# State-space phase powers for eight groups at once, one tap operand for real and imaginary part, the relu's square on ScalarE

## The chip, the core and the metric

The kernel runs on one core of a Trainium2 chip. Its time is the device time of one execution in microseconds (us). Engines are named as the profile names them: PE is TensorE's matmuls and PEld its weight loads, DVE is VectorE, ACT is ScalarE, POOL is GpSimd, SP is SyncE, which issues most of this kernel's transfers (DMA).

## The reference, cut to what matters

Two blocks of a network run one after the other on 512 tokens of width 1024, beside 256 context tokens. The change lies in the first block: in its squared-relu MLPs, and in what is prepared for the second layer's state-space (S5) mixer.

```python
def squared_relu_mlp(h, w1, w2):
    return jnp.square(jax.nn.relu(h @ w1)) @ w2

def s5_discretize(a_re, a_im, b_re, b_im, c_re, c_im, log_dt):
    ...
    a_bar = jnp.exp(dt * a)
    b_bar = ((a_bar - 1) / a)[..., None] * lax.complex(f(b_re), f(b_im))
    c_mat = lax.complex(f(c_re), f(c_im))
    return a_bar, b_bar, c_mat

def s5_scan(u, a_bar, b_bar, c_mat, x0):
    ...   # x[t] = a_bar * x[t-1] + b_bar u[t];  y[t] = Re(c_mat x[t]), 64 groups of 16 channels, 64 states
```

## The kernel before

**Stages.** In layer 0 a projection (w_out, `out_proj`, 8 column blocks) ends the first mixer; then comes the MLP of layer 0 (`mlp(0, ...)`) on all 768 tokens, the S5 mixer of layer 1, the MLP of layer 1 on 512 tokens, and the second network block. Each column block of a projection is one call of `lin`: a weight tile is loaded (SP), split into a high part `wh` (ACT, L250) and a low part `wl` (POOL, L258), and multiplied in three matmuls for each of 8 row blocks (L287, L288, L289), once for tokens 0 to 511 and once for 512 to 767. The results lie in PSUM tiles `mm`, four of them: two column blocks of 768 tokens.

**The MLP.** It goes in four quarters. A quarter makes 8 hidden tiles from w1 and then 8 column blocks of w2, whose results are added onto the stream by DVE (L507). A hidden tile is made for each token range from its `mm` tile: relu into `x` (ACT, L539), its square rounded into `fh` (ACT, L540), the full-precision square `max(mm, 0) * x` into `x` (DVE, L541, which reads `mm` again and so is the last to free it), and then, over both ranges, `fl = x - fh` (DVE, L258).

**S5 preparation.** While w_out and the MLP of layer 0 run, a generator does other work in small steps: `tick` is called after each `lin` and advances `background` by 91/66 of a step. Steps alternate between a column of layer 1's modulation (`ada`, DVE L377) and a step of `s5_prep`; after 32 columns all steps are `s5_prep`'s. It goes over 64 groups in fours (GB = 4), 16 passes, and for each pass:

- `ca`: powers times C, two complex products of 320 columns (24 DVE instructions with `pp` below); their imaginary part is negated (ACT, L695), both parts go to DRAM (`dQ`). Parts of both are copied into the zero-padded `z` (`s_cz`, ACT, L698 and L699), which has room for the real and the imaginary part. Eight matmuls `sw` (L704) multiply `z` by B: four with the real, four with the imaginary part, added in one PSUM tile.
- `W` (`s_w`): the tile evicted (ACT, L706), a diagonal added (DVE, L707), and sent to DRAM (`dT`) in 32 small transfers (SP, L710).
- `pp`: powers times B (DVE), transposed on PE into `st` (L721, real and imaginary part after each other), evicted into the one buffer `s_pt` (ACT, L722) and sent to DRAM (`dP`).
- `E` (`s_e`): the powers 0 to 96 of the unit phase, by doubling: seven complex products, each of six DVE instructions in `cmul` (L575 to L582), 4 groups by 1, 2, 4, 8, 16, 32 and 32 powers; then one transfer (`dE`).

The generator is empty after 66 of the 72 calls of `lin`. The S5 mixer begins with matmuls into `y` (L754), whose PSUM space is that of the preparation's tiles.

**Order.** The instructions' order on each engine is set when the program is built, by a scheduler that simulates times of its own; it runs over the whole program. On the chip each engine then goes in that order and waits where it has to.

Of the kernel before, what the change touches and what calls it, by code (L numbers as in the profile page):

```python
# [14 lines left out]
AF = mybir.ActivationFunctionType  # L15
OP = mybir.AluOpType
# [194 lines left out]
class Prog:  # L211
# [309 lines left out]
    def mlp(self, l, xs, nt, r, raw=None):  # L521
        nc = self.nc
        with ExitStack() as es:
            self.pp = es.enter_context(self.pool(f'psF{l}', space=PSUM, bufs=1))
            hp = es.enter_context(self.pool(f'hF{l}', side='right'))
            fp = es.enter_context(self.pool(f'hid{l}', side='right'))
            with ExitStack() as e2:
                self.slabs = 2
                hs = self.norm_mod(fp, hp, xs, nt, l, 1, r)
            for q in range(4):  # L530
                hid = []
                for u in range(8):
                    ps = self.lin(self.I['mlp_w1'][l, q * 8 + u], hs, nt)
                    r = self.slab(fp)
                    h = self.t(fp, [128, NT], 'fh', F32R, self.hid_bufs)
                    lo = self.t(fp, [128, NT], 'fl', F32R, self.hid_bufs)
                    for p, (g, o, n) in zip(ps, self.groups(nt)):
                        s = slice(o, o + n)
                        nc.scalar.activation(r[:, s], p[:, :n], AF.Relu)  # L539
                        nc.scalar.activation(h[:, s], r[:, s], AF.Square)  # L540
                        nc.vector.scalar_tensor_tensor(r[:, s], p[:, :n], 0.0, r[:, s], op0=OP.max, op1=OP.mult)  # L541
                    self.lo(lo[:, :nt], r[:, :nt], h[:, :nt])
                    hid.append((h, lo))
                st = Stat(self, [self.slab(fp) for _ in range(2)], nt) if q == 3 else None
                self.out_proj(self.I['mlp_w2'][l, q], hid, xs, nt, lambda c, g: self.mod[l][:, 40 + c, g:g + 1], st, raw if st else None)
            return st.end(fp)
# [37 lines left out]
    def s5_prep(self):  # L584

        nc, I, tc = self.nc, self.I, self.tc
        G = 64
        v = nc.vector
        sp = self.sp
# [11 lines left out]
        k = small('k')  # L601
# [60 lines left out]
        B = self.GB  # L662
# [4 lines left out]
        self.dR = dd('dR', [128, G])  # L667
        nc.sync.dma_start(self.dR, rho)
        self.dE = [dd(f'dE{i}', [128, 2, 8, 97]) for i in range(nb)]
        z = self.t(sp, [128, 2, B, 15, 16], 's_cz')  # L670
        nc.gpsimd.memset(z, 0.0)
        id16 = self.const('id16', pool=sp)
        N = 8
        bb = self.t(sp, [128, 2, N + 1, 16], 's_bb')
        nc.gpsimd.memset(bb[:, :, N], 0.0)
        yield
        for g0 in range(0, G, B):
            i, g8 = g0 // 8, slice(g0 % 8, g0 % 8 + B)
            g = slice(g0, g0 + B)
            if g0 % N == 0:  # L680
                b = self.t(sp, [128, 2, N, 16], 's_b')
                gn = slice(g0, g0 + N)
                nc.sync.dma_start(b, I['s5_b'][:, :, gn])
                bc = lambda x: x[:, gn, None].to_broadcast([128, N, 16])
                self.cmul(sp, (bb[:, 0, :N], bb[:, 1, :N]), (b[:, 0], b[:, 1]), (bc(cf[0]), bc(cf[1])), [128, N, 16], conj_tag='s_t')
                yield
            n0 = g0 % N
            c = self.t(sp, [128, 2, B, 16], 's_cc')
            nc.sync.dma_start(c, I['s5_c'][:, :, g])
            ca = self.t(sp, [128, 2, B, 10, 16], 's_ca')  # L690
            tk = lambda x: x[:, :, g].rearrange('p k g -> p g k')[:, :, :, None].to_broadcast([128, B, 10, 16])
            ck = lambda j: c[:, j, :, None, :].to_broadcast([128, B, 10, 16])
            for h in (slice(0, 5), slice(5, 10)):
                self.cmul(sp, (ca[:, 0, :, h], ca[:, 1, :, h]), (ck(0)[:, :, h], ck(1)[:, :, h]), (tk(PW[0])[:, :, h], tk(PW[1])[:, :, h]), [128, B, 5, 16], conj_tag='s_t')
            nc.scalar.activation(ca[:, 1], ca[:, 1], AF.Copy, scale=-1.0)  # L695
            for r in range(2):
                nc.sync.dma_start(self.dQ[i][:, r, g8], ca[:, r, :, 1:9].rearrange('p g t h -> p g (t h)'))
            nc.scalar.activation(z[:64, :, :, 7:], ca[:64, :, :, 0:8], AF.Copy)  # L698
            nc.scalar.activation(z[64:, :, :, :8], ca[64:, :, :, 2:10], AF.Copy)  # L699

            ps = ps_('sw')
            for r in range(2):
                for u in range(B):
                    nc.tensor.matmul(ps[32 * u:32 * u + 32, :240], bb[:, r, n0 + u:n0 + u + 2].rearrange('p g h -> p (g h)'), z[:, r, u].rearrange('p k h -> p (k h)'), start=r == 0, stop=r == 1)  # L704
            W = self.t(sp, [128, 15, 16], 's_w')
            nc.scalar.activation(W.rearrange('p t h -> p (t h)'), ps[:, :240], AF.Copy)  # L706
            v.scalar_tensor_tensor(W[:, 7], id16, self.pk('s5_d')[:, g0 // B:g0 // B + 1], W[:, 7], op0=OP.mult, op1=OP.add)  # L707
            for u in range(B):
                for s_ in range(8):
                    nc.sync.dma_start(self.dT[i][s_ * 16:s_ * 16 + 16, g0 % 8 + u], W[32 * u:32 * u + 16, 7 - s_:15 - s_].rearrange('p t h -> p (t h)'))  # L710
            yield
            pp = self.t(sp, [128, 2, B, 8, 16], 's_ca')
            tk = lambda x: x[:, :, g].rearrange('p k g -> p g k')[:, :, :, None].to_broadcast([128, B, 8, 16])
            ck = lambda j: bb[:, j, n0:n0 + B, None, :].to_broadcast([128, B, 8, 16])
            for h in (slice(0, 4), slice(4, 8)):
                self.cmul(sp, (pp[:, 0, :, h], pp[:, 1, :, h]), (ck(0)[:, :, h], ck(1)[:, :, h]), (tk(PP[0])[:, :, h], tk(PP[1])[:, :, h]), [128, B, 4, 16], conj_tag='s_t')
            for r in range(2):
                pt = self.t(sp, [128, B, 128], 's_pt')
                ps = ps_('st')
                for n in range(B):  # L720
                    nc.tensor.transpose(ps[:, n * 128:n * 128 + 128], pp[:, r, n].rearrange('p s h -> p (s h)'), self.ident)  # L721
                nc.scalar.activation(pt.rearrange('p g q -> p (g q)'), ps, AF.Copy)  # L722
                nc.sync.dma_start(self.dP[i][:, r, g8], pt)
            yield
            E = self.t(sp, [128, 2, B, 97], 's_e')
            nc.gpsimd.memset(E[:, 0, :, 0:1], 1.0)
            nc.gpsimd.memset(E[:, 1, :, 0:1], 0.0)
            for r in range(2):
                nc.gpsimd.tensor_copy(E[:, r, :, 1:2], ph[r][:, g, None])
            n = 1  # L730
            while n < 96:
                m = min(n, 96 - n)
                self.cmul(sp, [E[:, r, :, n + 1:n + 1 + m] for r in range(2)], [E[:, r, :, 1:1 + m] for r in range(2)],
                          [E[:, r, :, n:n + 1].to_broadcast([128, B, m]) for r in range(2)], [128, B, m], conj_tag='s_t')
                n += m
            nc.sync.dma_start(self.dE[i][:, :, g8], E)
            yield

    def s5_mixer(self, xs, xpx, x2x, r):
# [1388 lines left out]
```

## Time and profile before

| what | us |
|---|---|
| median of 3 timed runs (3776.2 to 3780.95) | 3779.33 |
| the profiled execution, its own time | 3774.4 |
| its span, first to last instruction | 3772.6 |
| PE busy (18415 matmuls) | 3457.0 (92%) |
| DVE busy (5101 instructions) | 2665.1 (71%) |
| ACT busy (2484) | 1531.7 (41%) |
| POOL busy (810) | 1263.9 (34%) |

The busy shares are means over stages that are limited by different things. So the profile is read by stage: for a stretch of time, how long each engine was busy, what PE waited for in it, and what clock PE was granted (1.00 is 2.4 GHz, 0.5 is 1.2 GHz).

### The profile page before, as it was taken

What the parts mean: (1) busy time and instruction counts of PE and PEld (TensorE: products, weight loads), DVE (VectorE), ACT (ScalarE), POOL (GpSimd) and SP (SyncE); (2) the same over time, 40 slices, a digit from 0 to 9 for tenths busy, and PEclk for the clock granted to TensorE, in tenths of its full rate; (3) what the DMA queues carried; (4) which work ended last, traced back from release to release, by engine and by line L of the source; (5) the groups of instructions that cost most, each with busy time, mean ns of one, the idle gap of its engine ahead of it and who ended that gap; (6) DMA issues with size and microseconds to landing.
All of it is one profiled execution on the core that took longest, in us unless ns stands there. A gap on an engine that the chain in (4) does not pass through costs nothing. (4 is left out here: it accounts for less than half of the span.)

```text
span 3772.6 us, 50694 instructions
## 1 busy us (share of the span) xinstructions
PE 3457.0 (92%) x18415; PEld 2923.8 (78%) x18415; DVE 2665.1 (71%) x5101; ACT 1531.7 (41%) x2484; POOL 1263.9 (34%) x810
## 2 busy tenths in 40 slices
PE   6889898999999778999999999899997699999998
PEld 4657667777888666788877987799997577799997
DVE  7895669877778796422278444599997677788864
ACT  4433563323323354322344444334778233333333
POOL 3663102222322354344445442322210332344420
PEclk9999898999999788999999999899999899999999
DMA  5442014344333453233332342335774999999981
GB/s 222 145 138 79 26 42 123 96 130 143 124 110 108 173 193 121 83 95 95 98 110 61 110 144 67 129 109 199 258 269 166 372 333 343 336 334 335 339 291 53
DMA packets 260585, 632.10 MB, mean 168 GB/s; under 512 B 39664, under 2 KB 124272, under 8 KB 257520
## 3 DMA queue, kind: packets, MB, share of 16 engines
q1 hardware_dynamic: 218832, 494.11, 38.7%
q0 software_dynamic: 36864, 134.23, 10.0%
q8 instruction: 145, 2.38, 0.3%
q10 hardware_dynamic: 4640, 0.53, 0.1%
q14 instruction: 104, 0.85, 0.1%
HBM read 547.65 MB, written 81.10 MB: 167 GB/s over the span
## 5 line engine op out<-in xcount | busy, mean ns | idle before, releaser
L258 POOL TENSOR_TENSOR wl<-wr,wh 128x1024 fp32r<-128x1024 f32 (+1 forms) x256 | 636.4, 2489 | 1061.4 <-ACT wh L250 995.3
L250 ACT ACTIVATE wh<-wr 128x1024 fp32r<-128x1024 f32 x328 | 346.3, 1056 | 643.1 <-PE mm L288 358.5
L287 PE MATMUL mm<-hh,wh 128*128 128x512 f32 (+1 forms) x1024 | 366.7, 363 | 25.1 <-DVE x L541 12.2
L288 PE MATMUL mm<-hl,wh 128*128 128x512 f32 (+1 forms) x1024 | 367.1, 359 | 1.8 <-DVE hl L351 1.7
L289 PE MATMUL mm<-hh,wl 128*128 128x512 f32 (+1 forms) x1024 | 365.9, 358 | 1.0 <-POOL wl L258 1.0
L287 PE MATMUL acc<-wh,ach 128*128 128x512 f32 x768 | 308.1, 405 | 59.1 <-ACT wh L250 34.4
L250 ACT ACTIVATE wh<-rw 128x1024 fp32r<-128x1024 f32 x184 | 195.1, 1060 | 374.9 <-PE acc L289 197.1
L287 PE MATMUL H<-wh,wh 128*128 128x384 f32 x1024 | 346.0, 338 | 0.0
L289 PE MATMUL H<-wh,wl 128*128 128x384 f32 x1024 | 345.6, 337 | 0.0
L288 PE MATMUL H<-wl,wh 128*128 128x384 f32 x1024 | 345.2, 337 | 0.0
L258 DVE TENSOR_TENSOR wl<-rw,wh 128x1024 fp32r<-128x1024 f32 x184 | 225.2, 1224 | 169.2 <-ACT wh L250 168.9
L288 PE MATMUL acc<-wl,ach 128*128 128x512 f32 x768 | 308.0, 401 | 0.0
L287 PE MATMUL mm<-fh,wh 128*128 128x512 f32 (+1 forms) x768 | 273.8, 357 | 5.3 <-DVE x L507 4.1
L288 PE MATMUL mm<-fl,wh 128*128 128x512 f32 (+1 forms) x768 | 274.6, 358 | 0.9 <-DVE fl L258 0.9
L1571 POOL DMA_INDIRECT rw<-in_p_v_dram,idx x127 | 156.4, 1231 | 350.2 <-DMA dGate<-Gs 107.4
L289 PE MATMUL mm<-fh,wl 128*128 128x512 f32 (+1 forms) x768 | 273.0, 356 | 0.0
L289 PE MATMUL acc<-wh,acl 128*128 128x512 f32 x768 | 252.1, 398 | 0.6 <-DVE acl L258 0.6
L287 PEld LDWEIGHTS mm<-hh,wh 128*128 128x128 f32 x1024 | 197.4, 194 | 64.2 <-DVE x L541 15.8
L288 PEld LDWEIGHTS mm<-hl,wh 128*128 128x128 f32 x1024 | 198.0, 193 | 34.2 <-DVE hl L351 3.5
L287 PEld LDWEIGHTS acc<-wh,ach 128*128 128x128 f32 x768 | 146.9, 192 | 96.2 <-ACT wh L250 34.6
L289 PEld LDWEIGHTS mm<-hh,wl 128*128 128x128 f32 x1024 | 197.2, 193 | 30.3 <-POOL wl L258 1.9
L287 PEld LDWEIGHTS H<-wh,wh 128*128 128x128 f32 x1024 | 192.5, 188 | 2.8
(688 smaller groups left out, 8524.1 us busy)
## 6 DMA issues: line engine op xcount, KB each, us to landing
wr<-in_mlp_w_dram SPq DMA_DIRECT2D x128, 512.0 KB, 3.6
rw<-in_p_v_dram SPq DMA_DIRECT2D x128, 512.0 KB, 6.4
wr<-in_p_ut_dram SPq DMA_DIRECT2D x72, 512.0 KB, 4.2
rw<-in_p_ut_dram SPq DMA_DIRECT2D x56, 512.0 KB, 5.8
aw<-in_ada_w_dram SPq DMA_DIRECT2D x48, 512.0 KB, 3.6
dGate<-Gs SPq DMA_DIRECT2D x48, 512.0 KB, 5.8
Gt<-dGate SPq DMA_DIRECT2D x32, 768.0 KB, 8.5
wr<-in_ada_w_dram SPq DMA_DIRECT2D x32, 512.0 KB, 4.3
```

The costliest lines, as they stand in the source:

```text
L250: self.nc.scalar.activation(dst, src, AF.Copy, **({} if scale is None else {'scale': scale}))
L258: e.tensor_tensor(dst, src, hi.bitcast(F32), op=OP.subtract)
L287: mm(out, ah, bh, start=first, stop=False)
L288: mm(out, ah, bl, start=False, stop=False)
L289: mm(out, al, bh, start=False, stop=last)
L1571: gp.indirect_dma_start(out=r, out_offset=None, in_=tab, in_offset=bass.IndirectOffsetOnAxis(ap=idx[:, s:s + 1], axis=0))
```

## The change

Three edits.

- In `mlp`, the DVE instruction L541 goes away. After the relu of both token ranges ACT squares `x` in place over all tokens, in full precision, and copies it, rounded, into `fh`. DVE's `fl = x - fh` stays.
- In `s5_prep`, `z` keeps one part only. ACT fills it with the real part, four `sw` matmuls read it, then ACT fills it with the imaginary part (which has to wait for these matmuls), and the other four read that.
- In `s5_prep`, `E` is formed once for eight groups, after the second of two passes, with instructions twice as wide; the step of `E` after the first pass goes away, and the step after the second is split in two behind power 64. The number of steps stays 57.

```diff
@@ mlp @@
                         nc.scalar.activation(r[:, s], p[:, :n], AF.Relu)
-                        nc.scalar.activation(h[:, s], r[:, s], AF.Square)
-                        nc.vector.scalar_tensor_tensor(r[:, s], p[:, :n], 0.0, r[:, s], op0=OP.max, op1=OP.mult)
+                    nc.scalar.activation(r[:, :nt], r[:, :nt], AF.Square)
+                    nc.scalar.activation(h[:, :nt], r[:, :nt], AF.Copy)
                     self.lo(lo[:, :nt], r[:, :nt], h[:, :nt])
@@ s5_prep @@
-        z = self.t(sp, [128, 2, B, 15, 16], 's_cz')
+        z = self.t(sp, [128, B, 15, 16], 's_cz')
...
-            nc.scalar.activation(z[:64, :, :, 7:], ca[:64, :, :, 0:8], AF.Copy)
-            nc.scalar.activation(z[64:, :, :, :8], ca[64:, :, :, 2:10], AF.Copy)
             ps = ps_('sw')
             for r in range(2):
+                nc.scalar.activation(z[:64, :, 7:], ca[:64, r, :, 0:8], AF.Copy)
+                nc.scalar.activation(z[64:, :, :8], ca[64:, r, :, 2:10], AF.Copy)
                 for u in range(B):
...
             yield
-            E = self.t(sp, [128, 2, B, 97], 's_e')
+            if g0 % 8 == 0:
+                continue
+            g = slice(g0 - B, g0 + B)
+            E = self.t(sp, [128, 2, 8, 97], 's_e')
...
                 n += m
-            nc.sync.dma_start(self.dE[i][:, :, g8], E)
+                if n == 64:
+                    yield
+            nc.sync.dma_start(self.dE[i], E)
             yield
```

The edits change the program that the scheduler sees, and with it the order. In the changed kernel lines behind the edits have numbers higher by five (the matmuls into `y` are L759), and L541 is ACT's copy. On PE, at the end of layer 0's MLP, there stood before (`mm` are the MLP's last matmuls, `bc` the sums for the next norm, `sw` and `st` the preparation's last pass, `y` the S5 mixer's first):

```order
L289 MATMUL mm_12550<-fh_12001,wl_12547 128x512
L287 MATMUL mm_12551<-fh_12001,wh_12546 128x256
L288 MATMUL mm_12551<-fl_12002,wh_12546 128x256
L289 MATMUL mm_12551<-fh_12001,wl_12547 128x256
L207 MATMUL bc_12603<-ones,x_12010 128x1 x6
L704 MATMUL sw_11956<-s_cz_4950,s_bb_4954 32x240 x8
L207 MATMUL bc_12603<-ones,x_12011 128x1 x6
L721 MATMUL st_12090<-c_ident_61,s_ca_12068 128x128 x4
L721 MATMUL st_12098<-c_ident_61,s_ca_12068 128x128 x4
L754 MATMUL y_12659<-c_ident_61,st_o_12625 128x128 x6
```

and now, on PE at the same place (the first half of `sw` stands 27 rows of matmuls ahead of the second):

```order
L704 MATMUL sw_11250<-s_cz_4950,s_bb_4954 32x240 x4
L288 MATMUL mm_11851<-fl_10987,wh_11846 128x256
...
L721 MATMUL st_11384<-c_ident_61,s_ca_11362 128x128 x4
L288 MATMUL mm_11910<-fl_10532,wh_11906 128x512
...
L721 MATMUL st_11392<-c_ident_61,s_ca_11362 128x128 x4
L289 MATMUL mm_11910<-fh_10986,wl_11907 128x512
...
L289 MATMUL mm_11911<-fh_11400,wl_11907 128x256
L207 MATMUL bc_11963<-ones,x_11407 128x1 x6
L207 MATMUL bc_11963<-ones,x_11408 128x1 x6
L759 MATMUL y_12019<-c_ident_61,st_o_11985 128x128 x6
```

The last pass's matmuls moved from behind the MLP into it: the second half of `sw` has 68 of the MLP's matmuls behind it and the last `st` 22.

On DVE, at the fifth hidden tile of the MLP's second quarter, there stood before (`s_ca`, `s_t`, `s_bb`, `s_ppr` and `s_ppi` belong to `pp`, `aj` to the modulation):

```order
L377 SCALAR_TENSOR_TENSOR aj_8244,modr_71<-wr_8242,cs_4729 128x1024
L577 TENSOR_TENSOR s_ca_7993<-s_t_1683_7994,s_t_1684_7995 128x4x64
L580 TENSOR_TENSOR s_t_1685_7999<-s_bb_4954,s_ppi_4888 128x256
L581 TENSOR_TENSOR s_t_1686_8000<-s_bb_4954,s_ppr_4887 128x256
L541 SCALAR_TENSOR_TENSOR x_7785<-mm_7731,x_7785 128x512
L582 TENSOR_TENSOR s_ca_7993<-s_t_1685_7999,s_t_1686_8000 128x4x64
L541 SCALAR_TENSOR_TENSOR x_7785<-mm_7732,x_7785 128x256
L575 TENSOR_TENSOR s_t_1687_8004<-s_bb_4954,s_ppr_4887 128x256
L576 TENSOR_TENSOR s_t_1688_8005<-s_bb_4954,s_ppi_4888 128x256
L258 TENSOR_TENSOR fl_7787<-x_7785,fh_7786 128x768
```

and now, on DVE at the same hidden tile:

```order
L576 TENSOR_TENSOR s_t_1591_7693<-s_bb_4954,s_ppi_4888 128x256
L377 SCALAR_TENSOR_TENSOR aj_7996,modr_71<-wr_7994,cs_4729 128x1024
L577 TENSOR_TENSOR s_ca_7681<-s_t_1590_7692,s_t_1591_7693 128x4x64
L580 TENSOR_TENSOR s_t_1592_7697<-s_bb_4954,s_ppi_4888 128x256
L581 TENSOR_TENSOR s_t_1593_7698<-s_bb_4954,s_ppr_4887 128x256
L258 TENSOR_TENSOR fl_7619<-x_7617,fh_7618 128x768
```

The two instructions that read `mm` are gone from DVE; no DVE instruction frees an `mm` tile of w1 any more.

On ACT, ahead of that tile, `z` (`s_cz`) is now filled in two pairs with other work between them:

```order
L701 ACTIVATE s_cz_4950<-s_ca_7477 64x4x128
L702 ACTIVATE s_cz_4950<-s_ca_7477 64x4x128
L540 ACTIVATE x_7549<-x_7549 128x768
L695 ACTIVATE s_ca_7477<-s_ca_7477 128x640
L541 ACTIVATE fh_7550<-x_7549 128x768
L701 ACTIVATE s_cz_4950<-s_ca_7477 64x4x128
L702 ACTIVATE s_cz_4950<-s_ca_7477 64x4x128
L539 ACTIVATE x_7617<-mm_7563 128x512
```

The second pair stands ahead of the next relu, and behind `sw`'s first half on PE.

## Rows read from the trace of the kernel before

**Rows 1.** Busy us (instructions) by stretch: PE, PEld, DVE, ACT, POOL; PE clock, DMA share, GB/s.

```profile
569.00:660.00 91.00, 75.19 (x424) 64.53 (x423) 84.58 (x212) 30.61 (x39) 21.27 (x14) 0.91 0.39 117
660.00:680.00 20.00, 18.65 (x101) 14.63 (x100) 19.93 (x47) 9.97 (x19) 0.00 (x0) 0.82 0.19 52
680.00:1276.00 596.00, 563.37 (x3311) 481.20 (x3310) 478.64 (x1185) 180.44 (x280) 166.30 (x119) 0.98 0.41 130
1276.00:1302.00 26.00, 7.82 (x53) 6.33 (x52) 14.71 (x62) 6.19 (x9) 2.62 (x1) 0.61 0.25 73
...
1603.10:1697.40 94.30, 94.30 (x410) 76.67 (x409) 22.26 (x27) 28.08 (x35) 40.84 (x17) 1.00 0.31 95
```

**Rows 2.** Waits from 680 to 1276 us: who for whom, total us, times, longest.

```profile
ACT s_pt L722 <- DMA dP<-s_pt: 57.5, 13, 10.5
...
PE mm L287 <- DVE x L541: 13.3, 10, 4.1
...
PE mm L287 <- DVE x L507: 8.0, 5, 3.9
...
PE st L721 <- DVE s_ca L577: 6.6, 3, 3.1
...
PE sw L704 <- ACT s_cz L699: 3.5, 3, 2.1
```

**Rows 3.** Timeline from 1276 us: start, length, engine and line, [idle before, releaser].

```profile
1276.15 1.39 PE L207 MATMUL bc<-ones,x 128*128 128x1 f32 x12
...
1278.73 1.02 PE L704 MATMUL sw<-s_cz,s_bb 128*32 128x240 f32 x16 [1.19 <-ACT s_cz L699]
...
1280.17 1.14 DVE L507 SCALAR_TENSOR_TENSOR x<-mm,mod,x 128x512 f32<-128x512 f32 x2
...
1283.70 14.90 SPq L710 DMA_DIRECT2D dT<-s_w  x32
...
1284.82 1.09 PE L721 MATMUL st<-c_ident,s_ca 128*128 128x128 f32 x4
...
1286.23 0.16 DVE L310 SCALAR_TENSOR_TENSOR st_o<-rs_a,rs_r 128x6 f32<-128x6 f32 x1
...
1286.60 1.11 PE L721 MATMUL st<-c_ident,s_ca 128*128 128x128 f32 x4 [0.69 <-ACT s_pt L722]
...
1298.70 0.37 SPq L723 DMA_DIRECT2D dP<-s_pt  x1
...
1300.88 0.60 ACT L722 ACTIVATE s_pt<-st 128x512 f32<-128x512 f32 x1 [14.34 <-DMA dP<-s_pt]
...
1301.53 1.54 PE L754 MATMUL y<-c_ident,st_o 128*128 128x128 f32 x6 [13.82 <-ACT s_pt L722]
```

**Rows 4.** Timeline of PE around 653 us, between w_out and the MLP.

```profile
653.48 2.72 PE L207 MATMUL bc<-ones,mr 128*128 128x1 f32 x12 [6.50 <-ACT mr L196]
```

**Rows 5.** DVE groups by shape, 569 to 1302 us: count, busy us, mean ns, idle before.

```profile
L541 DVE SCALAR_TENSOR_TENSOR x<-mm,x 128x512 f32<-128x512 f32 x32 | 21.9, 684 | 19.8 <-ACT fh L540 19.8
...
L581 DVE TENSOR_TENSOR s_t<-s_bb,s_ppr 128x256 f32<-128x256 f32 x32 | 13.3, 416 | 0.0
...
L541 DVE SCALAR_TENSOR_TENSOR x<-mm,x 128x256 f32<-128x256 f32 x32 | 13.3, 416 | 0.2
...
L581 DVE TENSOR_TENSOR s_t<-s_e 128x128 f32<-128x128 f32 x32 | 9.1, 283 | 0.0
...
L581 DVE TENSOR_TENSOR s_t<-s_e 128x4 f32<-128x4 f32 x16 | 2.5, 156 | 0.0
```

**Rows 6.** ACT groups by shape, 569 to 1302 us, the same columns.

```profile
L540 ACT ACTIVATE fh<-x 128x512 fp32r<-128x512 f32 x32 | 20.2, 632 | 0.0
...
L698 ACT ACTIVATE s_cz<-s_ca 64x1024 f32<-64x1024 f32 x16 | 16.9, 1057 | 0.4
...
L540 ACT ACTIVATE fh<-x 128x256 fp32r<-128x256 f32 x32 | 13.3, 418 | 0.1
...
L196 ACT ACTIVATE x<-x 128x768 f32<-128x768 f32 x8 | 6.7, 841 | 16.2 <-DVE x L507 16.0 <-DVE s_e L577 0.3
```

More of the change, by code (lines that the diff above doesn't have):

```diff
@@ L697, in s5_prep @@
                 nc.sync.dma_start(self.dQ[i][:, r, g8], ca[:, r, :, 1:9].rearrange('p g t h -> p g (t h)'))
-            nc.scalar.activation(z[:64, :, :, 7:], ca[:64, :, :, 0:8], AF.Copy)
-            nc.scalar.activation(z[64:, :, :, :8], ca[64:, :, :, 2:10], AF.Copy)
             ps = ps_('sw')
             for r in range(2):
+                nc.scalar.activation(z[:64, :, 7:], ca[:64, r, :, 0:8], AF.Copy)
+                nc.scalar.activation(z[64:, :, :8], ca[64:, r, :, 2:10], AF.Copy)
                 for u in range(B):
-                    nc.tensor.matmul(ps[32 * u:32 * u + 32, :240], bb[:, r, n0 + u:n0 + u + 2].rearrange('p g h -> p (g h)'), z[:, r, u].rearrange('p k h -> p (k h)'), start=r == 0, stop=r == 1)
+                    nc.tensor.matmul(ps[32 * u:32 * u + 32, :240], bb[:, r, n0 + u:n0 + u + 2].rearrange('p g h -> p (g h)'), z[:, u].rearrange('p k h -> p (k h)'), start=r == 0, stop=r == 1)
             W = self.t(sp, [128, 15, 16], 's_w')
@@ L733, in s5_prep @@
                 self.cmul(sp, [E[:, r, :, n + 1:n + 1 + m] for r in range(2)], [E[:, r, :, 1:1 + m] for r in range(2)],
-                          [E[:, r, :, n:n + 1].to_broadcast([128, B, m]) for r in range(2)], [128, B, m], conj_tag='s_t')
+                          [E[:, r, :, n:n + 1].to_broadcast([128, 8, m]) for r in range(2)], [128, 8, m], conj_tag='s_t')
                 n += m
-            nc.sync.dma_start(self.dE[i][:, :, g8], E)
+                if n == 64:
+                    yield
+            nc.sync.dma_start(self.dE[i], E)
             yield
```

## The prediction

> **What bounds the kernel now.** The profile is read first by stretch of time, since the busy shares of the whole span mix stages. In layer 1's MLP PE is busy for 94.30 of 94.30 us at full clock [rows 1]: whatever the first edit does to DVE and ACT there is worth nothing. The S5 preparation lies in another place, 569 to 1302 us. There w_out and layer 0's MLP run, and DVE is the crowded engine: busy for 84.58 of 91 us in w_out, 19.93 of 20 at the change to the MLP, 478.64 of 596 (80%) in the MLP [rows 1]. PE is still what the MLP consists of (563.37 of 596 us), but it is idle for 32.6 us, and its mean clock is 0.98, which is 2% of 563 or 11 us of work done at less than full clock.
>
> The second view is who waited for whom in those 596 us. PE waited 13.3 us for L541 (10 times), 8.0 us for L507, 6.6 us for the products of `pp` and 3.5 us for `z` [rows 2]. So most of PE's idle time is DVE being late, and the greatest part is the one instruction that the first edit takes off DVE.
>
> The third view is the timeline at the MLP's end. The MLP's last matmul ends at 1276.15, where the sums for the norm begin; the first matmul of the S5 mixer starts at 1301.53 [rows 3]. In these 25.4 us PE is busy for 7.82 [rows 1]. The norm itself is ready at 1286.23 (`st_o`). What ends last is the preparation's last pass: `sw` at 1278.73, the 32 transfers `dT` that hold SP's queue from 1283.70 for 14.90 us, behind them the transfer `dP` at 1298.70, whose landing lets ACT evict the second `st` at 1300.88, which frees the PSUM space of `y` [rows 3].
>
> **The change part by part.**
>
> *DVE work that goes.* L541 is 32 x (684 + 416) ns = 35.2 us in layer 0 [rows 5]. For `E`, one instruction takes 156 ns for 4 elements, 283 for 128 and 416 for 256 [rows 5]: about 152 ns and 1.03 ns an element. Its seven levels are 4, 8, 16, 32, 64, 128 and 128 wide before (380 in sum) and twice that now. A pass costs 6 x (7 x 152 + 380 x 1.03) = 8.7 us before, and a double pass 6 x (7 x 152 + 760 x 1.03) = 11.1 us: 16 x 8.7 - 8 x 11.1 = 51 us less. Together 86 us of the 583 that DVE is busy from 569 to 1276; in the MLP its share falls from 80% to about 67%.
>
> *ACT work that comes.* For 768 columns ACT takes 841 ns [rows 6]; square and copy are 2 x 841 for a hidden tile where the two squares were 632 + 418: 32 x 0.63 = 20 us more. `z` is four copies of 512 columns, at 632 each, for two of 1057: 16 x 0.41 = 7 us more. ACT is busy for 180 of 596 us in this stage [rows 1], so these 27 us are covered by its idle time; without that cover they would cost just that. The chain from `mm` to `fl` stays four instructions long. In layer 1 ACT gets some 20 us more and loses nothing but idle time. Half the `dE` transfers and of POOL's small copies go, which cost nothing where they stood.
>
> *Term 1, the end of the MLP.* In the new order the second half of `sw` stands 68 MLP matmuls ahead of the MLP's end. One matmul row of the MLP is 563.37 / 3311 = 0.17 us [rows 1]; with two `st` (about 0.6 us each at full clock, half of the 1.1 in rows 3) that is 12.8 us ahead. From `sw` to the first `dT` it was 5.0 us [rows 3]. So `dT` starts 7.8 us ahead of the end and leaves SP's queue 7.1 us behind it; `dP`'s landing (2.2 us from issue to L722) and the eviction (0.65) give `y` at 9.9. The norm needs, by the same rows, from L507 at 1280.17 to `st_o` at 1286.23, some 6 to 7 us. I take 9 us in place of 25.4, less some 2 us of `sw` and `st` that now lie inside the MLP: a gain of 14 us. Ends: 18 where only the norm is left, 6 where `dT` starts at the MLP's end (14.9 + 2.2 + 0.65 = 17.7 behind it).
>
> *Term 2, the change from w_out to the MLP.* PE waited 6.50 us for the last sums of the norm [rows 4], as DVE had the first pass's `E` in hand ahead of the last L507. In the new order no `E` stands there. DVE, full through 569 to 680 us, has 8.7 us less to do. Ends 0 and 9; I take 5, as the second pass's `ca` moves up into that place.
>
> *Term 3, inside the MLP.* Of the 13.3 us for L541 I take 11: an `mm` tile of w1 is now free after ACT's relu, and ACT goes through these with time in hand, but it too stops (57.5 us for `dP` in 13 waits) [rows 2]. Of the 14.6 us for L507 and `pp` I take 6, for a DVE with a sixth less work. The clock gives back 2 of 11 us. Against this stands the new wait: ACT fills `z` a second time only after `sw`'s first half, PE's second half waits for that, and on ACT the next relu, square and weight split queue behind it. In 15 of 16 passes 27 to 32 matmul rows (4.6 us or more) lie between the halves, and the fill is 1.3 us, so I take 4 us in all. Nothing in the trace shows this wait; its bounds are 0, and 16 times a third of the mean wait for `dP` (4.4 us), 23 us. Term 3: 11 + 6 + 2 - 4 = 15 us, ends -8 and 28.
>
> *A rule beside rows 5 and 6.* The Trainium skill (ScalarE: Activation LUTs, Rules for kernel authors) tells to use VectorE, not ScalarE, for relu, max and mul, which speaks against the first edit. Here ACT's square of 512 takes 632 ns and DVE's product 684, so the rows don't bear it out for this shape. Were L541's removal worth nothing, term 3 would be 4 and the time 3756.
>
> *A rule beside rows 5.* The Trainium skill (VectorE: DVE Perf Modes, The TRN2 errata) gives a fixed cost for each instruction and then one for each element; it has 58 cycles where the rows show 152 ns. By its figure, an estimate, the `E` edit saves 20 us of DVE in place of 51, and the time would be some 3 us later.
>
> **Sum.** 14 + 5 + 15 = 34 us off the profiled execution's 3774.4 (span 3772.6 and 1.8 around it) is 3740.4. That execution was 4.9 us below the median of 3779.33; set against the median the forecast is 3745.
>
> **The rivals.**
>
> *A, the relief doesn't reach PE.* DVE and ACT also stop for transfers queued behind `dT` in SP's queue (the 57.5 us above), and `dT` has 16 x 32 issues as before. Then terms 2 and 3 are near nothing and term 1 is its lower end, 6: 3773, within the bound of no change. For it: ACT's waits are longer in sum than PE's. Against it: PE's ten waits are for L541, which is gone.
>
> *B, slower: the split `z` stops PE.* On ACT other waits, above all L722's for `dP`, can stand between the two fills; then PE stands at `sw`'s second half. Were each of 15 passes to cost one mean wait for `dP`, 4.4 us, that is 66 us, beyond the 4 already counted 62, and the time 3779 - 34 + 62 = 3807. It decides from 34 / 15 = 2.3 us a pass on. Against it: the scheduler has put the halves apart, and PE waited for `z` only 3.5 us in three waits so far [rows 2].
>
> *C, all ends at the good side:* 18 + 9 + 28 = 55 us, 3724. [...] Against it: the waits on transfers remain.
>
> That the change doesn't do what it says is no rival: the new order has 336 narrow products and 96 L541 fewer on DVE.
>
> **How the numbers follow.** Forecast (3732 to 3768): 0.70. A: 0.13. B: 0.08. C: 0.09. About 0.2% (7.6 us) is what a measurement of this kernel can tell from no change. Faster by more: the forecast, C, and little else, 0.80; same: most of A, 0.12; slower: B, 0.08. The range takes in C's edge and most of the way to A: 3722 to 3771.
>
> **What would show it.** Right: from the MLP's last matmul to the first `y` some 9 us, with `dT` begun ahead of that end; no PE wait for a DVE line in w1's column blocks; DVE busy for some 67% there; layer 1's MLP unchanged. Wrong: PE waits at `sw` of more than 2 us a pass; `y` still released by `s_pt` 20 us behind the MLP; or PE's waits named L539 or L541 of ACT, which would make ACT the late engine.

## The result, and the profile after

| what | before | after |
|---|---|---|
| median of the timed runs, us | 3779.34 (3776.2 to 3780.95) | 3739.76 (3736.31 to 3744.39) |
| ratio, 95% interval | | 0.9896 (0.988 to 0.9912) |
| the profiled execution, span | 3772.6 | 3742.6 |
| DVE busy in it (instructions) | 2665.1 (5101) | 2563.6 (4669) |
| ACT busy in it (instructions) | 1531.7 (2484) | 1582.4 (2548) |

The change takes 39.6 us, 1.0%. The forecast was 3745, 34 us less than before. In a second series on another chip the changed kernel took 3742.89 us, ratio 0.9902 (0.9886 to 0.9919). The total came as forecast; the runs below show that its parts did not.

To compare the two traces, the time from w_out's first matmul to the S5 mixer's first is cut at three events that both have: w_out's last matmul, the spread of the norm's result on PE (L319) and the MLP's last matmul. These are the busy times of each stretch, in the columns of [rows 1], of the kernel before:

```profile
565.05:645.80 80.75, 74.41 (x411) 63.36 (x411) 73.56 (x183) 27.76 (x35) 18.35 (x9) 0.94 0.39 117
645.80:659.20 13.40, 3.92 (x24) 3.76 (x23) 12.12 (x31) 4.67 (x7) 2.92 (x5) 0.66 0.56 174
659.20:1276.30 617.10, 583.11 (x3417) 496.93 (x3417) 499.67 (x1231) 191.51 (x298) 166.30 (x119) 0.97 0.40 128
1276.30:1301.50 25.20, 7.05 (x49) 5.56 (x47) 14.40 (x61) 5.89 (x9) 2.62 (x1) 0.60 0.22 68
```

and of the changed kernel:

```profile
567.02:647.70 80.68, 74.94 (x411) 63.80 (x411) 71.24 (x160) 28.31 (x37) 18.45 (x9) 0.92 0.38 116
647.70:656.50 8.80, 5.50 (x41) 4.05 (x39) 5.92 (x12) 7.25 (x11) 2.36 (x1) 0.69 0.52 150
656.50:1252.50 596.00, 578.51 (x3424) 491.26 (x3425) 436.39 (x917) 222.02 (x328) 159.28 (x91) 0.98 0.42 133
1252.50:1259.90 7.40, 4.00 (x26) 3.86 (x24) 6.80 (x17) 2.70 (x4) 2.35 (x1) 0.68 0.17 54
```

The change from w_out to the MLP is 4.6 us shorter, the MLP 21.1, the end of the MLP 17.8: 43.6 us together. PE's idle time in the MLP went from 34.0 us (617.10 less 583.11) to 17.5. Behind the first `y` the changed kernel's profiled execution is 11.6 us longer than that of before (2482.7 against 2471.1), though the instructions there are the same but for layer 1's relu; this gets a paragraph of its own below. With w_out's first matmul 2.0 us later, the two traces are 30.0 us apart and not 39.6: each is one execution, that of before 4.9 us under its kernel's median and that of the changed kernel 4.6 over.

The waits in the changed kernel's MLP (who for whom, total us, times, longest) answer to [rows 2]:

```profile
ACT s_pt L722 <- DMA dP<-s_pt: 48.9, 12, 6.7
PE mm L287 <- ACT fh L541: 4.7, 1, 4.7
PE st L721 <- DVE s_ca L577: 3.5, 3, 1.7
PE sw L704 <- ACT s_cz L702: 2.8, 3, 1.4
PE mm L287 <- DVE x L507: 1.3, 2, 0.8
```

PE's 13.3 us for L541 are gone, those for L507 fell from 8.0 to 1.3, and PE waits 2.8 us for `z` where it waited 3.5. ACT still waits 48.9 us for `dP`. The longest wait of PE is now one of 4.7 us, for ACT's L541, the copy into `fh`.

The MLP's end in the changed kernel (start, length, engine and line), which answers to [rows 3]:

```profile
1241.38 15.55 SPq L710 DMA_DIRECT2D dT<-s_w  x32
...
1252.37 1.40 PE L207 MATMUL bc<-ones,x 128*128 128x1 f32 x12
...
1257.03 0.37 SPq L723 DMA_DIRECT2D dP<-s_pt  x1
...
1259.13 0.60 ACT L722 ACTIVATE s_pt<-st 128x512 f32<-128x512 f32 x1 [0.22 <-DMA dP<-s_pt]
...
1259.57 0.17 DVE L310 SCALAR_TENSOR_TENSOR st_o<-rs_a,rs_r 128x6 f32<-128x6 f32 x1
...
1259.88 1.51 PE L759 MATMUL y<-c_ident,st_o 128*128 128x128 f32 x6 [1.41 <-DVE st_o L310]
```

The 32 transfers `dT` start 11.0 us ahead of the sums for the norm (L207) and are out 4.6 us behind the start of these, so that the last eviction (L722) and the norm (`st_o`) end together, and `y` now follows the norm.

### The profile page after: what moved, and what is told of

Read it like the earlier page. It is cut to its first block, busy times and chain, and to the rows that moved or that the text cites. A ratio compares the mean times of both kernels' runs of the same rounds, so it can differ in the third digit from the quotient of the medians.

```text
span 3742.6 us, 50317 instructions
## 1 busy us (share of the span) xinstructions
PE 3460.0 (92%) x18415; PEld 2920.7 (78%) x18415; DVE 2563.6 (68%) x4669; ACT 1582.4 (42%) x2548; POOL 1255.7 (34%) x778
```

## The experiments

Each kernel was run beside the kernel before; its ratio is to that. The prices of the stretches come from each kernel's trace, cut as above (the first column runs from w_out's first matmul to L319). "Taps once" stands for `W` sent in one transfer a pass, "POOL in halves" for each weight split made in two instructions; both are shown below.

| kernel | us | to L319 | MLP | its end | from `y` on |
|---|---|---|---|---|---|
| before | 3777.8, 3776.1, 3779.4 in the three series | 94.1 | 617.1 | 25.2 | 2471.1 |
| relu's square alone | 3778.95 | 95.9 | 617.6 | 14.2 | 2485.7 |
| single `z` alone | 3750.01 | 92.7 | 599.4 | 15.8 | 2475.0 |
| four short copies, two `z` | 3774.26 | 95.2 | 615.1 | 19.0 | 2475.9 |
| single `z` and `E` for eight | 3740.41 | 89.2 | 600.1 | 7.6 | 2474.8 |
| changed kernel | 3739.76 | 89.5 | 596.0 | 7.4 | 2482.7 |
| changed kernel, second series | 3742.89 | 89.4 | 596.2 | 7.4 | 2481.3 |
| before, taps once | 3771.95 | 93.6 | 627.4 | 4.7 | 2479.2 |
| single `z`, `E`, taps once | 3740.01 | 89.6 | 598.6 | 4.8 | 2479.2 |
| changed, taps once | 3729.46 | 89.8 | 589.6 | 5.6 | 2472.9 |
| before, POOL in halves | 3764.44 | 92.0 | 606.8 | 28.5 | 2467.7 |
| single `z`, POOL in halves | 3738.24 | 90.1 | 592.4 | 16.3 | 2471.3 |
| changed, POOL in halves | 3734.03 | 92.9 | 590.2 | 8.9 | 2473.3 |
| changed, taps once, POOL in halves | 3725.88 | 89.9 | 586.7 | 4.7 | 2479.3 |

### The three edits apart

The theory was the prediction's: the relu's edit brings the gain inside the MLP, `E` for eight the ends, and the single `z` costs a little. The room in SBUF allows `E` for eight only together with the single `z`, so `E` alone was not tried.

```diff
 # e1_phase_tap: the changed kernel, with the old relu
-                    nc.scalar.activation(r[:, :nt], r[:, :nt], AF.Square)
-                    nc.scalar.activation(h[:, :nt], r[:, :nt], AF.Copy)
+                        nc.scalar.activation(h[:, s], r[:, s], AF.Square)
+                        nc.vector.scalar_tensor_tensor(r[:, s], p[:, :n], 0.0, r[:, s], op0=OP.max, op1=OP.mult)
```

> The change without its first edit: E for eight groups and one z, but L541 stays on DVE. (E for eight groups without the smaller z finds no room in SBUF, so the two go together.) Theory, by the prediction's terms: the end of the MLP (14 us) and the change from w_out (5) come from E, and of what is inside the MLP the 6 us for L507 and pp, less 4 us for the new wait: 21 us, some 3758. PE's waits for L541 stay near 13 us, 7.5 to 10 us pass from the MLP's last matmul to the first y. Rival, all the gain is DVE's load and so is shared by DVE time removed (51 of 86 us): 24 us here, 3756, but with the waits for L541 well below 13 us. Rival, the gain is L541 alone: 3770 or more.

Measured: 3740.41 us, ratio 0.9901 (0.9886 to 0.9916). All of the gain is there without the relu's edit, and none of the three expectations had that.

The relu's edit alone (e2_square, the first hunk of the change on the kernel before):

> The first edit alone: relu, square and copy on ACT, E in fours and z with both parts as before. Theory: no PE wait for a DVE line in w1's column blocks, 11 us plus about 1 of clock from there; in this order the last sw stands 45 matmul rows ahead of the MLP's end, so the 32 transfers dT begin about 3 us ahead of it and y comes about 14 to 15 us behind it in place of 25.4: another 8 to 10. Together some 20 us, 3759. Rival, DVE's late work was only uncovered by L541 and PE then waits for L507 and pp in its place: under 8 us of gain, 3772 to 3779. The two parts' gains add up to the whole change's 39.6 within 8 us if the terms are separate.

Measured: 3778.95 us, ratio 0.9994 (0.9984 to 1.0003): nothing, as the rival said, though the MLP's end is 11.0 us shorter in its trace. PE's waits in its MLP:

```profile
PE mm L287 <- DVE x L507: 10.5, 5, 4.7
PE st L721 <- DVE s_ca L577: 6.7, 3, 3.1
PE sw L704 <- ACT s_cz L699: 6.4, 4, 3.7
PE mm L287 <- ACT fh L541: 5.2, 1, 5.2
```

The 13.3 us for L541 are gone, and the waits for L507, `z` and the new `fh` have grown by 2.5, 2.4 and 5.2: the MLP takes 617.6 us as against 617.1. DVE's work there did fall, from 499.67 to 482.81 us. The one wait of 5.2 us for `fh` has a cause outside DVE:

```profile
890.80 15.00 SPq L710 DMA_DIRECT2D dT<-s_w  x32
...
905.90 0.37 SPq L723 DMA_DIRECT2D dP<-s_pt  x1
...
908.00 0.60 ACT L722 ACTIVATE s_pt<-st 128x512 f32<-128x512 f32 x1 [10.61 <-DMA dP<-s_pt]
...
909.12 0.83 ACT L541 ACTIVATE fh<-x 128x768 fp32r<-128x768 f32 x1
```

ACT stood for 10.61 us at L722 until `dP` had landed, which was issued behind the 32 `dT`, and the copy into `fh` that PE waited for came after it.

The single `z` alone (e3_tap, the second hunk):

> The second edit alone: z with one part at a time, all else as before. Theory: the new wait costs what the prediction took, 4 us, with PE's wait at sw up from 3.5 us to 5 to 10 us, and 3779 to 3787. Rival B of the prediction, in which the split stops PE: 15 to 60 us slower, 3795 to 3840, with PE's wait at sw of more than 2 us a pass. Rival, it costs nothing since the scheduler puts the halves apart: within 3 us of before.

Measured: 3750.01 us, ratio 0.9922 (0.9908 to 0.9935). The edit that was priced as a loss is the greatest gain of the three. It takes 17.7 us out of the MLP and 9.4 out of its end, and `E` for eight on top of it another 9.6 of the total. PE's waits in its MLP:

```profile
PE mm L287 <- DVE x L541: 6.3, 4, 2.7
PE sw L704 <- ACT s_cz L702: 4.4, 4, 2.0
PE st L721 <- DVE s_ca L577: 4.3, 2, 3.3
```

No wait for L507 is left, and L541's have halved, though DVE is busy for as long as before (501.33 us against 499.67).

### Why the single z helps: the copies, or the one buffer

The edit does two things: it cuts the fills into four copies of 512 columns, and it makes the second half of `sw` wait for the first. One kernel has the first alone.

```diff
 # e7_halves_two_z, on the kernel before; z keeps both parts
-            nc.scalar.activation(z[:64, :, :, 7:], ca[:64, :, :, 0:8], AF.Copy)
-            nc.scalar.activation(z[64:, :, :, :8], ca[64:, :, :, 2:10], AF.Copy)
             ps = ps_('sw')
             for r in range(2):
+                nc.scalar.activation(z[:64, r, :, 7:], ca[:64, r, :, 0:8], AF.Copy)
+                nc.scalar.activation(z[64:, r, :, :8], ca[64:, r, :, 2:10], AF.Copy)
```

> The kernel before with the fills of z cut in four copies of 512 columns, the real part's two ahead of its four products, the imaginary part's two ahead of the other four, but with both parts of z kept, so that no fill waits for a product. Theory 'short copies': the 28 us of the single z come from ACT being held 1.26 us at a time in place of 2.1 and from the real part being filled ahead of the negation L695; both are here, so some 3750 to 3756. Rival 'spacing': they come from the wait itself, which puts the second half of sw some 27 matmuls behind the first and moves the preparation's later products against w2's accumulations; it isn't here, so 3772 to 3780. In between would mean that each brings a part.

Measured: 3774.26 us, ratio 0.9996 (0.9987 to 1.0005). PE's waits in its MLP:

```profile
PE mm L287 <- DVE x L541: 14.8, 12, 2.7
PE mm L287 <- DVE x L507: 7.1, 5, 3.8
```

So the short copies are worth nothing. What is left is the one buffer: the wait that it makes, and the order that the scheduler builds around that wait, which these runs don't tell apart. The traces show one place where the order differs and PE's wait with it, the fifth hidden tile of the MLP's second quarter, which stands in the order of DVE ahead of the prediction. In the kernel before:

```profile
875.40 1.23 DVE L377 SCALAR_TENSOR_TENSOR aj<-wr,cs 128x1024 bf16<-128x1024 f32 x1 [2.69 <-DMA wr<-in_ada_w_dram]
...
875.90 5.47 POOL L258 TENSOR_TENSOR wl<-wr,wh 128x1024 fp32r<-128x1024 f32 x2 [9.80 <-ACT wh L250]
...
876.55 2.61 DVE L577 TENSOR_TENSOR s_ca<-s_t,s_t 128x256 f32<-128x256 f32 x1
...
879.19 2.45 DVE L580 TENSOR_TENSOR s_t<-s_bb,s_ppi 128x256 f32<-128x256 f32 x1
...
881.91 0.68 DVE L541 SCALAR_TENSOR_TENSOR x<-mm,x 128x512 f32<-128x512 f32 x1
...
882.64 0.79 PE L287 MATMUL mm<-hh,wh 128*128 128x512 f32 x1 [4.09 <-DVE x L541]
```

Two products of `pp` that take 0.41 us elsewhere take 2.61 and 2.45 us while POOL makes two weight splits (5.47 us), L541 stands behind them, and PE waits 4.09 us for it. The same tile with the single `z`:

```profile
862.73 2.40 POOL L258 TENSOR_TENSOR wl<-wr,wh 128x1024 fp32r<-128x1024 f32 x1 [5.71 <-ACT wh L250]
...
863.00 3.21 DVE L377 SCALAR_TENSOR_TENSOR aj<-wr,cs 128x1024 bf16<-128x1024 f32 x1 [0.69 <-DMA wr<-in_ada_w_dram]
...
866.15 1.01 DVE L541 SCALAR_TENSOR_TENSOR x<-mm,x 128x512 f32<-128x512 f32 x2
```

Here nothing stands between `aj` and L541, and PE doesn't wait. Counted over the MLP, PE has ten waits of 0.5 us or more for L507 or L541 in the kernel before, and three with the single `z`. Nine of the ten have a lengthened DVE instruction (over 0.5 us longer than the quick ones of its form) in the 9 us ahead of them; in the tenth, 3.7 us at 688 us, L541 itself came late because it waited for ACT's L540. By itself this count says little, since at 68% of all times in this MLP a lengthened instruction stands in the 9 us before. With the single `z` as many instructions are lengthened (48, by 95.4 us in sum, against 51 by 99.8), and PE waits behind fewer of them. Why the scheduler's order comes out so with one buffer is not shown by any run.

### Is it POOL that makes DVE late?

```diff
 # e10_pool_halves, on the kernel before, in weight()
-        self.lo(l[:, :n], raw[:, :n], h[:, :n], lo_eng)
+        for o in ((0, n // 2), (n // 2, n)) if lo_eng == 'pool' and n == 1024 else ((0, n),):
+            self.lo(l[:, o[0]:o[1]], raw[:, o[0]:o[1]], h[:, o[0]:o[1]], lo_eng)
```

> The kernel before with each weight split of 1024 columns on POOL (2.4 us) made in two instructions of 512. In layer 0's MLP some 50 of DVE's products last 2 us longer than their like, 100 us in sum, each of them beside one of POOL's 64 splits. Theory 'POOL holds DVE up': DVE gets in between the halves, the sum falls to about half, and with it a third to a half of PE's 28 us of waits for DVE: 3764 to 3770. Rival 'DVE is late by its own amount of work': the same sum in more and shorter pieces, 3775 to 3782, or slower by POOL's added instructions.

Measured: 3764.44 us, ratio 0.997 (0.9958 to 0.9982), the MLP 10.3 us shorter. POOL's splits in the MLP (count, busy us, mean ns), before:

```profile
L258 POOL TENSOR_TENSOR wl<-wr,wh 128x1024 fp32r<-128x1024 f32 x63 | 158.1, 2509 | 378.1 <-ACT wh L250 339.5 <-DMA dP<-s_pt 31.3 <-DMA dT<-s_w 7.3
```

and in halves:

```profile
L258 POOL TENSOR_TENSOR wl<-wr,wh 128x512 fp32r<-128x512 f32 x125 | 174.5, 1417 | 352.9 <-ACT wh L250 345.4 <-PE sw L705 7.4
```

Before, 51 of DVE's instructions last over 0.5 us longer than the quick ones of the same form; all 51 overlap a split of POOL, and the mean excess is 1.96 us. In halves it is 80 instructions, all beside a split, with a mean excess of 0.99 us, half of what it was, as POOL's instruction takes 1.42 us in place of 2.51. The sum fell less than expected, to 79 us and not to half. PE's idle time in the MLP fell from 34.0 to 25.0 us: the waits for L507 from 8.0 to 2.9 and those for `pp` from 6.6 to 1.7, while those for L541 stayed at 13.3. So POOL does hold DVE up, and PE pays for part of it; how much of the gain is the new order that comes with the halves was not tried apart.

Does the single `z` only avoid these waits, so that both together bring no more?

> The single z alone (3750.0) and POOL's weight split in two halves (3764.4 by itself, 11.7 less than before). In the trace of before, ten of PE's waits for L507 and L541 have a DVE product lengthened by 2 us beside a split of POOL just ahead of them; with the single z three are left. Theory 'same waits': the single z took away most of the waits that the halves would shorten, so that the two overlap: 3744 to 3750. Rival 'two sources': the halves give what they gave before, 11 us or more: 3739 or less.

Measured: 3738.24 us, ratio 0.9891 (0.9875 to 0.9908): 11.8 us less than the single `z` alone, as much as the halves gave before. "Same waits" falls for the total. But PE's idle time in the MLP is the same with and without halves (17.0 and 17.3 us); of the 7.0 us that the MLP is shorter, 6.7 are PE's busy time, 575.47 against 582.13 us at a clock of 0.99 against 0.98, and 3.6 us more come in the 580 us behind layer 1's MLP. On the changed kernel:

> The changed kernel (3739.8) and POOL's weight split in two halves. In its trace of the MLP only two waits of PE for L507 are left, 1.3 us in sum, and none for L541. 'Same waits': little is left inside the MLP, 3734 to 3741, of which some 4 us from the stages behind it. 'Two sources': 3728 or less.

Measured: 3734.03 us, ratio 0.9885 (0.9868 to 0.9901), at the lower end of "same waits". By the trace 5.8 us are gained in the MLP and 9.4 behind `y`, and 3.4 lost ahead of the MLP and 1.5 at its end.

### SP's queue

The prediction's rival A said that the 32 transfers `dT` of a pass hold what follows them in SP's queue. In the next kernels `W` goes out in one transfer, and the mixer reads it with 8 loads:

```diff
 # e6_before_taps_once, on the kernel before
-            for u in range(B):
-                for s_ in range(8):
-                    nc.sync.dma_start(self.dT[i][s_ * 16:s_ * 16 + 16, g0 % 8 + u], W[32 * u:32 * u + 16, 7 - s_:15 - s_].rearrange('p t h -> p (t h)'))
+            nc.sync.dma_start(self.dT[i][g0 % 8 // B], W.rearrange('p t h -> p (t h)'))
```

> The kernel before, with one cost taken away: W is sent to DRAM in one transfer a pass in place of 32 (16 in place of 512), and its eight shifted copies are made when the S5 mixer loads T (8 transfers of its own for each T, in place of 1). If the queue of SP behind dT sets the end of the MLP, y comes 8 to 10 us behind the MLP's last matmul in place of 25.4, and ACT's wait for dP (57.5 us) falls below 15 us: 15 us or more of gain, 3764 or less. If DVE sets it, the end shrinks by less than 6 us and PE's waits for L541 and L507 stay at 21 us: 3773 or more. The S5 mixer may give back up to 3 us by the 56 further loads.

Measured: 3771.95 us, ratio 0.9986 (0.9977 to 0.9995). The MLP's end falls by 20.5 us to 4.7, so `dT` did hold it; but the last passes move into the MLP, which grows by 10.3 us, and from `y` on 8.1 more are lost. The total lies between the two expectations. On top of the single `z` and `E`:

> The phase powers for eight groups and the single z (3740.4 by itself), and the tap matrix W sent in one transfer a pass in place of 32, with T built by 8 loads where it is used. Theory 'SP's queue still counts': with the single z in place the waits of ACT for dP (some 50 us in 12 waits) go, and 6 us or more come on top: 3734 or less. Rival 'the end is bounded by the norm by now': the last st already lies ahead of the MLP's end, so nothing is left at the end (2.8 us there at most), and the passes that the scheduler then packs closer bring their waits inside the MLP as they did without the single z (10 us there): 3738 to 3748.

Measured: 3740.01 us, ratio 0.9901 (0.9886 to 0.9917), no gain, as the rival said. On the changed kernel:

> The changed kernel and the tap matrix sent in one transfer a pass. By the theory 'SP's queue still counts' 3734 or less; by the rival 3738 to 3748. Against the run without the relu's edit in the same call it tells once more what that edit is worth: by the two times so far 0 to 1 us, by the traces of the MLP alone 4.

Measured: 3729.46 us, ratio 0.9878 (0.9863 to 0.9893), 10.6 us less than the run without the relu's edit in the same series, whose time no run of this one reaches. Set against each series' own kernel before, the one transfer pays 7 to 10 us beside the relu's edit and nothing without it. With POOL in halves as well:

> The changed kernel, the tap matrix in one transfer a pass (3729.5) and POOL's split in halves: the version that should be best if both are worth something. 'Same waits': 3724 to 3731. 'Two sources': 3719 or less.

Measured: 3725.88 us (3723.72 to 3730.14), ratio 0.9855 (0.9839 to 0.9872), 53.5 us less than before and the best of all, within "same waits". It beats the changed kernel; against taps once alone the intervals overlap. ACT's waits for `dP` in the MLP are down to 6.6 us, and those for `st` on PE take their place:

```profile
ACT s_pt L721 <- PE st L720: 44.6, 15, 4.1
...
ACT s_pt L721 <- DMA dP<-s_pt: 6.6, 2, 5.0
```

### What is given back behind the MLP

The relu's edit was taken three times: on the kernel before, on the single `z` with `E`, and on that with taps once. From w_out to `y` it brings 8.8, 4.0 and 8.0 us in the traces. From `y` on it costs 14.6 and 7.9, and in the third case gains 6.3. The medians differ by +1.2, -0.7 and -10.6 us, the profiled executions as a whole by +7.3, +6.7 and -13.8: in the first two cases the single traces show 6 to 7 us more of loss than the medians. What is given back is partly clock. The first 15 us behind layer 1's MLP, with the same instructions and the same 14.22 us of busy PE, and then the whole stretch up to the first matmul into `H`, some 580 us, in the kernel before:

```profile
1914.80:1929.80 15.00, 14.22 (x74) 10.77 (x72) 5.66 (x12) 10.10 (x14) 5.20 (x6) 1.00 0.53 173
1914.80:2496.10 581.30, 547.74 (x2952) 466.97 (x2951) 349.07 (x817) 244.30 (x380) 244.21 (x156) 0.95 0.31 100
```

and with the relu's edit alone:

```profile
1911.50:1926.50 15.00, 14.22 (x67) 10.13 (x66) 5.66 (x12) 8.54 (x12) 5.19 (x6) 0.89 0.48 146
1911.50:2501.90 590.40, 554.26 (x2953) 472.80 (x2952) 349.13 (x817) 244.03 (x381) 244.12 (x156) 0.93 0.31 98
```

At a granted clock of 0.89 PE gets through 67 matmuls where it does 74 at 1.00; over the stretch PE is busy 6.5 us longer at 0.93 than at 0.95. The changed kernel was run again to see whether that stays:

> The changed kernel once more, beside the others on one chip, and a second trace of it. By the two times so far 3736 to 3744. In its first trace the 15 us behind layer 1's MLP ran at a granted clock of 0.89, where the kernels before, single z and single z with eight groups have 1.00 for the same instructions, and the stretch from there to the first product of H took 586.8 us against 581 to 582. Theory 'belongs to the program': 0.89 again. Rival 'belongs to the execution': 1.00 and 581 to 583 this time.

Measured: 3742.89 us, and in its trace:

```profile
1874.80:1889.80 15.00, 14.22 (x66) 10.15 (x65) 5.65 (x12) 8.53 (x12) 5.20 (x6) 0.89 0.44 148
1874.80:2458.50 583.70, 549.19 (x2953) 467.61 (x2952) 349.65 (x817) 244.34 (x381) 246.22 (x156) 0.95 0.31 99
```

The 0.89 at this place belongs to the program. It isn't the relu's edit as such: the two kernels with taps once on top of the single `z` have it too, and one of them has the old relu. The whole stretch was 586.8 us in the first trace and 583.7 in this one, so that part of the loss changes from one execution to the next. Nor does the 0.89 of these 15 us make up the loss: the changed kernel with taps once has it and takes 582.9 us for the stretch, against 581.3 before. The kernels' times from `y` on lie between 2467.7 and 2485.7 us for nearly the same instructions; why one program gets the lower clock there and another doesn't stays open.

## Why the prediction came out as it did

**The total** held: 39.6 us where 34 were forecast, inside the range. In part that is luck. The traces show 43.6 up to `y` and 11.6 given back behind it, where the prediction had 34 and nothing, and the largest piece of term 3 was put down to an edit that brings nothing by itself.

**Term 1, the end of the MLP,** was right in mechanism and size: 7.4 us are left where 9 were taken. `dT` started 11.0 us ahead of the end, not 7.8. The step named one cause, the new order; the runs show that each edit's own order shortens the end: the single `z` alone by 9.4 us, `E` on top of it by 8.2 more, and the relu's edit alone by 11.0.

**Term 2, the change from w_out,** was right: 4.6 us of 5. PE's wait of 6.50 us [rows 4] is 0.26. It came in two steps: the transition is 13.4 us long before, 11.5 with the single `z` alone (PE's wait 3.74) and 8.8 with `E` for eight as well.

**Term 3, inside the MLP,** is the step that failed in its parts. It gave 15 us (13 after the 2 us of `sw` and `st` that moved in), and 21.1 were measured, but from another edit.
- *11 us for L541*: the ten waits did go, but the relu's edit alone left the MLP as long as it was, since other waits of PE's took their place, the longest of them for ACT's `fh`. Beside the other two edits it is worth 4.1 us there, and 9.0 with taps once. Nor were all ten DVE's lateness: for the one of 3.7 us, DVE itself stood idle for 1.55 us until ACT's L540 was done.
- *6 us for a DVE with less work*: `E` for eight takes DVE from 501.33 to 467.83 us in the MLP, and the MLP's time doesn't move (599.4 and 600.1). DVE's share of the MLP is 73% and not 67%. The work was priced well: `E`'s instructions from w_out to `y`, added up, are 185.4 us before (672) and 123.5 after (336). In these sums 43 and 33 us are the excess of lengthened instructions; without it they fall by 52, where 51 were forecast. The Trainium skill (VectorE: DVE Perf Modes, The TRN2 errata) says below the table row of 58 cycles, from which the prediction got 20, that this row comes out too short, and has (N + 151)/0.96 ns for a float32 `tensor_tensor` of N columns; by that the estimate is 53 us, and the trace agrees. But the amount of work was not what PE waited for.
- *4 us lost to `z`*: PE waits 2.8 us for `z` where it waited 3.5, so nothing was lost; what the step missed is that the edit also changes the order of the work around it. Alone it takes 17.7 us out of the MLP. The prediction read in the two orders that L541 was gone and where `sw` stood, and not what stood ahead of each L507 and L541 elsewhere.
- *2 us of clock*: the MLP's mean clock went from 0.97 to 0.98, and PE's busy time fell by 4.6 us.

What stood behind this: the rows of [rows 5] are means. In the MLP the trace of before has, for the same shape (count, busy us, mean ns, idle time):

```profile
L577 DVE TENSOR_TENSOR s_ca<-s_t,s_t 128x256 f32<-128x256 f32 x28 | 24.1, 861 | 24.6 <-DMA dQ<-s_ca 13.9 <-ACT wh L250 6.1 <-issue 1.8
...
L581 DVE TENSOR_TENSOR s_t<-s_bb,s_ppr 128x256 f32<-128x256 f32 x28 | 11.7, 417 | 0.0
```

Two operations of one shape with 861 and 417 ns: this was the sign that a fifth of DVE's busy time, 100 of 500 us, was not work but the excess of instructions beside a split of POOL. A prediction that had asked for it would have looked at where the lengthened ones stand ahead of L507 and L541.

**The signs.** `y` came 7.4 us behind the MLP's last matmul, with `dT` begun ahead of it; in w1's column blocks PE waited for DVE only 1.7 us, for the norm's `hl` at the start; layer 1's MLP took 358.1 us against 356.9, with PE busy throughout. One sign of being wrong came too: PE's longest wait names ACT's L541 (4.7 us), but once only.

**The rivals.** A (the relief doesn't reach PE) describes the relu's edit taken alone, and in part by its own reason: PE's longest new wait, 5.2 us, ends a chain that begins with `dT` in SP's queue. With one transfer in place of 32 the relu's edit brings 9.0 us in the MLP, and 10.6 in the total. For the whole change A did not hold: ACT's waits for `dP` stayed near 50 us and PE's went. B (the split `z` stops PE) did not come; PE waits 2.8 us in three of the passes. C, all ends at the good side, did not come either: its ends add up to 55 us, and the traces show 43.6 up to `y`, of which the stages behind it took a quarter back.

**The rule against ScalarE** (the Trainium skill, ScalarE: Activation LUTs, Rules for kernel authors) gave 3756. ACT's square and copy of 768 columns take 849 and 846 ns, as priced. The relu's edit alone did bring nothing, but not because these instructions are slow on ACT: ACT stood waiting for `dP` ahead of the copy that PE needed. With taps once the edit brings 10.6 us.

## What to carry to other kernels

Price an edit by what PE waits for behind it, not by the engine's busy time it saves: here 33 us less of DVE's busy time changed the MLP by nothing, and an edit that left that time as it was changed it by 18. Where two instructions of one shape have different means on one engine, find out what runs beside the slow ones before calling the time work. An edit that a scheduler sees is also a change of order, so take each edit by itself before saying which one paid, and read the stages behind it, where a few microseconds can go back.

## What the hardware showed that was not expected

DVE's products of two SBUF operands stop while POOL makes a two-operand instruction: 51 of 51 lengthened ones in the MLP stand beside a split of 2.5 us, with 1.96 us of excess on the mean, and 0.99 us where the split is 1.4 us long. All 51 began while a split was running, and 48 of them ended 0.02 to 0.8 us behind that split's end. L541, which reads `mm` in PSUM and one operand in SBUF, is never longer than 692 ns in all of its 96 instances in the kernel before, of which 42 began while a split was running:

```profile
L541 DVE SCALAR_TENSOR_TENSOR x<-mm,x x96: 409/683/692, 687.5 to 1873.3; 128x512 f32<-128x512 f32 x64, 128x256 f32<-128x256 f32 x32
```

The Trainium skill (SBUF — State Buffer, SBUF: two separate sides) says that DVE and GpSimd share one pair of ports as an exclusive lock, which a DVE instruction with two SBUF inputs needs and which the one that starts first keeps for its whole instruction. The trace agrees: of the products that overlap a split and are not lengthened, 30 of 45 began ahead of it and 11 in its last 0.45 us. Its price in this kernel is seen with POOL's splits halved: the kernel before is 11.7 us faster, though POOL's splits of the MLP take 174.5 us in place of 158.1.
